# Keys of a gated recurrence transposed by VectorE blocks and a way through DRAM, not by TensorE

## The chip, the cores and the metric

The kernel runs on one core of one Trainium2 chip. Its metric is the device time of one execution in microseconds. The runs shown here and the profile are of that one core; the profile is of one execution, taken by the hardware profiler.

## The reference

One layer of a streaming encoder on a sequence of 2048 positions with 1024 channels, in float32:

```python
xn = rmsnorm(x, norm1_g)
u_pool, zq, zf, zi, zo, zg = split(xn @ w_in)          # 512 columns each, zg 2048
gates = sigmoid(zg + b_gate)
ya = pool_mixer(u_pool, pool_w, pool_scale) @ w_pa      # causal means over 2, 4, 8, 16 positions
yb = hgrn2_mixer(zq, zf, zi, zo, lower_bounds, g) @ w_pb
x = x + (gates[0] * ya + gates[1] * yb) @ w_o
x = x + conv_glu_ffn(rmsnorm(x, norm2_g), w_up, conv_w, conv_b, w_down)
return rmsnorm(x, final_g)
```

The change is in `hgrn2_mixer`, a linear recurrence with four heads of 128 channels and a forget gate f per position and channel:

```python
q = silu(zq); f = lb + (1 - lb) * sigmoid(zf); k = 1 - f; v = zi
S_t = diag(f_t) S_(t-1) + k_t^T v_t                     # S is 128 x 128
o_t = S_t^T q_t
```

It is computed in chunks of positions: inside a chunk by products of decayed q and k, from chunk to chunk through S. For the state, a chunk of 128 positions adds the matrix product of its decayed keys and its values, summed over the positions. Then o is normalised per head and multiplied with silu(zo).

## The kernel before, in words

**Projections.** Nearly all of TensorE's time is in large products (line 149), which are done in parts by a fast matrix scheme: a unit of four output tiles has the banks `X`, `Z` and `V` of PSUM, into which products of sums and differences of blocks go. Each product is done three times, with the high and low parts of both operands (`x_f6h`, `x_f6l`), and a matmul has 512 columns. ACT and DVE make the two parts of each weight tile (`ops`, lines 245 and 246); DVE takes the sums out of the banks (`gr_u` from `gr_Z`, line 1234, and so on), after which a bank is written again.

**Stages.** The sequence is worked in two halves (b = 0 and 2), each with two blocks of 512 positions. For each half come the input projection, the two branch projections, the output projection, and after both the feed-forward layer. The recurrence runs beside the input projection's units: `hgrn_task` is a Python generator, called for 4 blocks and 4 heads (16 times). Three runners work through the queue of such tasks. After every six projection matmuls the program takes a tick, in which each waiting generator counts down; `yield 4` means four ticks. So the recurrence's small products lie between projection matmuls in the program's order. A scheduler then fixes each engine's order once, when the kernel is built, by its own estimate of times; on the chip each engine goes strictly through its list and waits where an operand isn't there.

**A head.** A tile is 128 partitions by 512 elements, four chunks (`NT = 4`) of 128 positions. In `ks` the 128 channels lie on the partitions and the positions along the row. Levels of doubling (lines 1051 to 1127) multiply q, k and f and fill the matrix `att` inside the chunk. Then the keys are needed with positions on the partitions, since the state's product sums over them: TensorE transposes each chunk of `ks` into the bank `pk` (line 1131) by a product with the identity, and ACT copies the bank to `kt` (1133). The state products `pv` (line 1140) have a chunk of `kt` as the stationary operand, loaded into the array, and the chunk of `vt` as the moving one. An FP32 product takes two passes. DVE makes the states `ss` one after the other (line 1148), the last of a block into `st`. The outputs `po` sum the product inside the chunk (`v`, `att`, line 1156) and that of the state (`st` or `ss`, `q`, line 1158). Lines 1163 to 1178 normalise, transpose back (`pt`) and store (`od`).

**Queues.** SP issues all loads of weights (`raw`, line 198), the stores of combined weights (`wb<-cw`, line 983, rows of 512 bytes, two of 128 KB each; `kw..<-raw`), and the loads of heads (`v`, `z`, line 999). `spill` stores from ACT's queue, and `fetch` (lines 990 to 993) loads by default from SP's. At the end of a half the pooled channels come back as `mx` (line 992), and DVE makes the parts of `mf..` from them (lines 681 and 1503).

Of the kernel before, what the change touches and what calls it, by code (L numbers as in the profile page):

```python
# [11 lines left out]
F32 = mybir.dt.float32  # L12
# [6 lines left out]
P = 128  # L19
# [10 lines left out]
TB = 512  # L30
NT = TB // P
# [51 lines left out]
def tile_trunk(  # L83
# [16 lines left out]
    pe, act, dve, pool, sp = nc.tensor, nc.scalar, nc.vector, nc.gpsimd, nc.sync  # L100
# [6 lines left out]
    dram = ctx.enter_context(tc.tile_pool(name="dram", bufs=1, space=bass.MemoryType.DRAM))  # L107
    banks = ctx.enter_context(tc.tile_pool(name="banks", bufs=8, space=bass.MemoryType.PSUM))

    def slot(name, cols=TB, dt=F32):  # L110
        return slots.tile([P, cols], dt, tag="s", name=name, padded_shape=[P, 528])

    def bank(name, cols=512):
        return banks.tile([P, cols], F32, tag="b", name=name, padded_shape=[P, 512])
# [470 lines left out]
    ident = const.tile([P, P], F32, tag="ident", name="ident")  # L585
# [404 lines left out]
    def fetch(d, name, eng=sp):  # L990
        t = slot(name)
        eng.dma_start(t, d)  # L992
        return t


    def hgrn_task(b, h, d, q, vd, zd, od):
        def head_of(src, key):
            t = slot(f"{key}{b}_{h}")
            sp.dma_start(t.rearrange("p (c v) -> p c v", c=NT), src[:, :, h * P : (h + 1) * P])
            return t  # L1000

        vt = head_of(vd, "v")
        ks = slot(f"k{b}_{h}")
# [78 lines left out]
        for lv in (0, 1, 2, 4, 6):  # L1082
# [42 lines left out]
            dve.tensor_tensor(k3[:, :, 0, :], k3[:, :, 0, :],  # L1125
                              d3[:, :, 1, 0:1].to_broadcast(full), ALU.mult)
            dve.tensor_tensor(d3[:, :, 0, 0:1], d3[:, :, 0, 0:1], d3[:, :, 1, 0:1], ALU.mult)
        yield 4
        pk = bank(f"pk{b}_{h}")
        for c in range(NT):  # L1130
            pe.transpose(pk[:, c * P : (c + 1) * P], ks[:, c * P : (c + 1) * P], ident)
        kt = slot(f"kt{b}_{h}")
        act.copy(kt, pk)
        yield 4
        while (b, h) not in state_at:
            yield 1
        zt = head_of(zd, "z")
        pv = bank(f"pv{b}_{h}")
        for c in range(NT):
            pe.matmul(pv[:, c * P : (c + 1) * P], kt[:, c * P : (c + 1) * P],  # L1140
                      vt[:, c * P : (c + 1) * P], start=True, stop=True)
        ss = slot(f"ss{b}_{h}")
        par = b % 2
# [32 lines left out]
        t = slot(f"oh{b}_{h}")  # L1176
# [224 lines left out]
    def mixer(b0, forms, late):  # L1401
# [16 lines left out]
        def runner():  # L1418
            while taken[0] < 2 * HEADS:
                if queue:  # L1420
                    taken[0] += 1
                    yield from hgrn_task(*queue.pop(0))
                else:
                    yield 1
# [575 lines left out]
```

## Time and profile before

| What | Value |
|---|---|
| Time, median of 3 runs | 2505.35 us (2504.9 to 2505.46) |
| Span of the profiled execution, first to last instruction | 2503.3 us |
| Mean granted TensorE clock | 0.999 |
| TensorE busy | 2490.4 us (99%), 11428 matmul instructions |
| VectorE busy | 1977.8 us (79%) |
| ScalarE busy | 1201.1 us (48%) |
| GpSimd busy | 805.1 us (32%) |
| Transposes of the keys, line 1131 | 64, from 170.2 to 1661.6 us |
| State products, line 1140 | 128 passes, from 176.7 to 1676.3 us |

The profile's page gives the busy time of each engine, the chain that ended last, groups of instructions by line, and the DMAs with their time from issue to landing. TensorE's matmuls are pipelined: what one costs is the distance from its start to the next start, which the timelines show, and not its duration. In a name such as `pv<-v,kt` the tile ahead of the arrow is written, those behind are read. A row of waits says which engine stood idle at which line for whom: microseconds in all, times, the longest.

### The profile page before, as it was taken

How to read it: one execution, taken by the hardware profiler on the slowest of the kernel's cores; microseconds unless marked ns; L12 is line 12 of the kernel's file. 1: busy time of each engine (PE TensorE's matmuls, PEld its weight loads, DVE VectorE, ACT ScalarE, POOL GpSimd, SP SyncE). 2: the span in 40 equal slices, each digit the busy share in tenths (PEclk: the TensorE clock that was granted, in tenths of full speed). 3: DMA queues.
4: the chain of work that ended last, by engine and by line, in shares of the span. 5: the costliest groups of instructions: out<-in, count | busy, mean ns of one | idle time of the engine just before them, and what ended most of it. 6: DMA issues, size and time to landing. Idle time of an engine off the chain costs nothing.

```text
span 2503.3 us, 35640 instructions
## 1 busy us (share of the span) xinstructions
PE 2490.4 (99%) x11428; PEld 2039.1 (81%) x11428; DVE 1977.8 (79%) x3510; ACT 1201.1 (48%) x2264; POOL 805.1 (32%) x1139
## 2 busy tenths in 40 slices
PE   9999999999999999999999999999999999999998
PEld 7888888888888888888888888887888888888887
DVE  7778768997998778885596777679979887778755
ACT  6534443435555545553554344443365555445534
POOL 4343353403354333451320202223033433325410
PEclk9999999999999999999999999999999999999999
DMA  8888788688888789897344343447443454447852
GB/s 276 271 206 247 227 229 242 210 243 251 202 255 238 226 228 243 263 366 244 122 152 152 118 127 110 143 141 259 135 148 122 153 150 138 149 137 247 319 165 100
DMA packets 257691, 497.68 MB, mean 199 GB/s; under 512 B 26912, under 2 KB 47520, under 8 KB 257184
## 3 DMA queue, kind: packets, MB, share of 16 engines
q1 hardware_dynamic: 189872, 317.53, 40.0%
q0 software_dynamic: 42656, 112.74, 17.7%
q10 hardware_dynamic: 24976, 65.13, 7.5%
q8 instruction: 90, 1.47, 0.2%
q14 instruction: 97, 0.79, 0.1%
HBM read 383.63 MB, written 189.27 MB: 229 GB/s over the span
## 4 chain that ended last, share of the span: by engine, by line
PE 97%; DVE 1%; ACT 0%; DMA 0%; issue 0%; POOL 0%; SPq 0%; ACTq 0%; DVEq 0%
PE dn_P L149 17%; PE up_Z L149 15%; PE up_X L149 10%; PE up_V L149 10%; PE wo_P L149 6%; PE gr_Z L149 5%; PE gr_X L149 4%; PE gr_V L149 4%; PE pb L149 4%; PE io_Z L149 3%; PE fr_Z L149 3%; PE fr_X L149 2%; PE fr_V L149 2%; PE io_V L149 2%; PE pl L1057 2%; PE ur_Z L149 1%
## 5 line engine op out<-in xcount | busy, mean ns | idle before, releaser
L245 ACT CAST ops<-raw 128x512 fp32r<-128x512 f32 x792 | 489.3, 621 | 826.4 <-PE dn_P L149 176.6
L246 DVE TENSOR_TENSOR ops<-raw,ops 128x512 fp32r<-128x512 f32 x792 | 590.4, 749 | 202.8 <-ACT ops L245 198.4
L1734 DVE SCALAR_TENSOR_TENSOR e<-h,cols,e 128x512 f32<-128x512 f32 x176 | 143.4, 819 | 30.9 <-ACT e L1732 23.7
L1732 ACT ACTIVATE e<-h,cols 128x512 f32<-128x512 f32 x176 | 142.2, 814 | 25.1 <-DVE h L1190 18.2
L1737 DVE SCALAR_TENSOR_TENSOR e<-h,cols,e 128x512 f32<-128x512 f32 x176 | 134.0, 771 | 2.5
L992 POOL DMA_DIRECT2D g_P<-dg_P x154 | 83.8, 545 | 160.7 <-PE dn_P L149 112.1
L1303 POOL TENSOR_TENSOR gf_P<-e,e 128x512 f32<-128x512 f32 x44 | 61.1, 1391 | 149.4 <-DVE e L1743 95.9
L467 POOL TENSOR_TENSOR raw<-raw,raw 128x512 f32<-128x512 f32 x36 | 49.1, 1363 | 157.6 <-DVE ops L246 124.5
L1303 POOL TENSOR_TENSOR gf_P<-gf_P,e 128x512 f32<-128x512 f32 x44 | 59.2, 1345 | 71.8 <-DVE e L1743 71.4
L1727 POOL COPY h<-h 128x2 f32<-128x2 f32 x88 | 40.5, 472 | 117.3 <-DVE h L1189 110.4
L1443 POOL TENSOR_TENSOR q<-q,qs 128x512 f32<-128x512 f32 x16 | 22.1, 1380 | 166.3 <-ACT qs L1442 163.9
L1741 ACT ACTIVATE e<-e 128x512 f32<-128x512 f32 x88 | 55.6, 632 | 39.6 <-DVE e L1737 39.3
L1729 POOL COPY hist<-h 128x2 f32<-128x2 f32 x88 | 35.3, 402 | 118.9 <-DVE h L1190 117.1
L1190 DVE TENSOR_TENSOR h<-up_u,up_V 128x512 f32<-128x512 f32 x88 | 60.1, 683 | 10.2 <-PE up_V L149 9.7
L1278 DVE TENSOR_TENSOR x<-x,wo_P 128x512 f32<-128x512 f32 x88 | 56.0, 684 | 6.7 <-PE wo_P L149 6.3
L1476 ACT ACTIVATE gt<-gt,cols 128x512 f32<-128x512 f32 x48 | 34.9, 726 | 53.1 <-DVE gt L1190 39.5
L1278 DVE TENSOR_TENSOR ac<-ac,dn_P 128x512 f32<-128x512 f32 x72 | 47.1, 683 | 16.7 <-PE dn_P L149 16.3
L1042 POOL COPY qm<-q 128x64 f32<-128x64 f32 x64 | 27.1, 446 | 98.4 <-DVE q L1048 19.9
L1228 ACT COPY up_e<-up_X 128x512 f32<-128x512 f32 x44 | 25.8, 587 | 59.5 <-PE up_X L149 52.3
L1727 POOL COPY h<-hist 128x2 f32<-128x2 f32 x88 | 45.1, 519 | 28.5 <-DVE m_T42l L681 28.5
L1757 POOL DMA_DIRECT2D dg_P<-gf_P x88 | 50.7, 576 | 8.1 <-POOL gf_P L1303 7.4
L1057 PE MATMUL pl<-qm,k 128*128 128x192 f32 x256 | 50.0, 325 | 0.0
(1335 smaller groups left out, 8061.8 us busy)
## 6 DMA issues: line engine op xcount, KB each, us to landing
g_P<-dg_P POOLq DMA_DIRECT2D x154, 256.0 KB, 6.2
raw<-in_w_up_t SPq DMA_DIRECT2D x132, 256.0 KB, 3.3
raw<-in_w_in_t SPq DMA_DIRECT2D x98, 256.0 KB, 3.6
dg_P<-gf_P POOLq DMA_DIRECT2D x88, 256.0 KB, 4.0
dg_P<-e SPq DMA_DIRECT2D x66, 256.0 KB, 3.5
raw<-in_w_dn SPq DMA_DIRECT2D x66, 256.0 KB, 3.8
x<-in_x SPq DMA_DIRECT2D x64, 256.0 KB, 5.2
gd<-gt ACTq DMA_DIRECT2D x64, 256.0 KB, 2.7
```

The source lines that it names most:

```text
L149: count[1] = pe.matmul(*args, **kw)
L245: self.mark = act.copy(hi, v)
L246: low = self.low = dve.tensor_tensor(lo, v, f32(hi), ALU.subtract)
L992: eng.dma_start(t, d)
L1057: ins = pe.matmul(pa_[:, c * 192 : c * 192 + 192], ks[:, (i + c) * P : (i + c + 1) * P], mv[:, c].rearrange("p s x -> p (s x)"), start=Tru ...
L1190: return dve.tensor_tensor(dst, t, ps, ALU.add if how == "add" else ALU.subtract)
L1278: dve.tensor_tensor(t, t, ps[j], ALU.add if sg > 0 else ALU.subtract)
L1303: pin(eng.tensor_tensor(t, x0, x1, op))
L1727: pool.tensor_copy(h[:, 0:2], hist[:, mt] if hf == 0 else hs[s, 0][:, TB : TB + 2])
L1732: in_turn(act.activation(t, h[:, 2:], AF.Identity, bias=col(o_cb + mt), scale=col(o_cw + 4 * MF + mt)))
L1734: in_turn(second(dve.scalar_tensor_tensor(t, h[:, 1 : 1 + TB], col(o_cw + 2 * MF + mt), t, ALU.mult, ALU.add)))
L1737: dve.scalar_tensor_tensor(t, h[:, 0:TB], col(o_cw + mt), t, ALU.mult, ALU.add)
```

## The change

`pk` and the copy to `kt` go. In their place:

1. `blocks_turned`: one DVE instruction transposes the tile in blocks of 32x32, 64 blocks in a tile. It reads runs of 32 and writes with a stride of four elements (16 bytes), so that one chunk's blocks lie in every fourth element.
2. `blocks_moved`: four DMAs on SP's queue store the tile to a new DRAM tile `kd`, 64 KB each, a group of 32 partitions at a time, in runs of 512 bytes. The rows are put so that the DRAM tile holds the full transpose.
3. `fetch`: one DMA on SP's queue loads `kd` as `kt`, 256 KB in rows of 2 KB. The view `"p (m c) -> p c m"` takes chunk c as every fourth element.
4. The state product's stationary operand is `kt[:, c]`: 128 elements, 16 bytes from one to the next. The moving operand is the same as before.

The ticks around it are 2, 2, 2 and 3 in place of 4 and 4. In all 16 heads: 64 transposes of TensorE and 16 copies of ScalarE out, 16 transposes of VectorE and 80 DMAs on SP's queue (64 stores, 16 loads) in.

```diff
--- before.py
+++ after.py
@@ -993,6 +993,19 @@
         return t
 
 
+    def blocks_turned(t, name):
+
+        z = slot(name)
+        dve.transpose(z.rearrange("p (b j c) -> p b c j", b=4, c=NT),
+                      t.rearrange("p (c b i) -> p b c i", c=NT, b=4))
+        return z
+
+    def blocks_moved(dst, z, eng=sp):
+
+        d = dst.rearrange("(b i) (a m) -> a i b m", b=4, a=4)
+        for a in range(4):
+            eng.dma_start(d[a], z[32 * a : 32 * a + 32].rearrange("i (b m) -> i b m", b=4))
+
     def hgrn_task(b, h, d, q, vd, zd, od):
         def head_of(src, key):
             t = slot(f"{key}{b}_{h}")
@@ -1125,19 +1138,20 @@
             dve.tensor_tensor(k3[:, :, 0, :], k3[:, :, 0, :],
                               d3[:, :, 1, 0:1].to_broadcast(full), ALU.mult)
             dve.tensor_tensor(d3[:, :, 0, 0:1], d3[:, :, 0, 0:1], d3[:, :, 1, 0:1], ALU.mult)
-        yield 4
-        pk = bank(f"pk{b}_{h}")
-        for c in range(NT):
-            pe.transpose(pk[:, c * P : (c + 1) * P], ks[:, c * P : (c + 1) * P], ident)
-        kt = slot(f"kt{b}_{h}")
-        act.copy(kt, pk)
-        yield 4
+        yield 2
+        kz = blocks_turned(ks, f"kz{b}_{h}")
+        yield 2
+        kd = dram.tile([P, TB], F32, tag=f"kd{b}_{h}", name=f"kd{b}_{h}")
+        blocks_moved(kd, kz)
+        yield 2
+        kt = fetch(kd, f"kt{b}_{h}").rearrange("p (m c) -> p c m", c=NT)
+        yield 3
         while (b, h) not in state_at:
             yield 1
         zt = head_of(zd, "z")
         pv = bank(f"pv{b}_{h}")
         for c in range(NT):
-            pe.matmul(pv[:, c * P : (c + 1) * P], kt[:, c * P : (c + 1) * P],
+            pe.matmul(pv[:, c * P : (c + 1) * P], kt[:, c],
                       vt[:, c * P : (c + 1) * P], start=True, stop=True)
         ss = slot(f"ss{b}_{h}")
         par = b % 2
```

The orders of the engines move with it. The names: a number behind `pv`, `kt`, `ss`, `po` is the block and the head (`pv1_3` is block 1, head 3); `gr0_7_Z` is a bank of the last unit of the input projection, `mf0..` and `mx..` the pooled channels. Lines behind 1008 are 13 or 14 higher in the changed kernel (1140 is 1154, 1148 is 1162, 1156 and 1158 are 1170 and 1172, 1234 is 1248, 1503 is 1517).

First TensorE at the end of the first half's input projection, before, from the last head's state product on. Behind the last of these rows follow 21 more of line 149, then the remaining `po` products, the first of which reads `ss`:

```order
L1140 MATMUL pv0_3_4656<-v0_3_4057,kt0_3_4582 128x128 x4
L149 MATMUL gr0_7_V_4631<-x1_T13l_774,ops130_4511 128x512
L149 MATMUL gr0_7_V_4631<-x1_T13h_773,ops130_4511 128x512
L1156 MATMUL po0_3_4727<-v0_3_4057,at0_3_4062 128x128
L1158 MATMUL po0_3_4727<-st3_0_128,q0_3_4018 128x128
L1156 MATMUL po0_3_4727<-v0_3_4057,at0_3_4062 128x128
L1140 MATMUL pv1_3_4747<-v1_3_4071,kt1_3_4589 128x128 x2
L149 MATMUL gr0_7_Z_4595<-x1_T30h_819,ops131_4541 128x512
```

The same place of TensorE after:

```order
L149 MATMUL gr0_7_X_4579<-x0_f7h_419,ops132_4584 128x512
L1154 MATMUL pv0_3_4685<-v0_3_4069,kt0_3_4639 128x128 x4
L1170 MATMUL po0_3_4756<-v0_3_4069,at0_3_4074 128x128
L1172 MATMUL po0_3_4756<-st3_0_128,q0_3_4030 128x128
L1170 MATMUL po0_3_4756<-v0_3_4069,at0_3_4074 128x128
L1154 MATMUL pv1_3_4776<-v1_3_4083,kt1_3_4641 128x128 x4
L1172 MATMUL po0_3_4756<-ss0_3_4690,q0_3_4030 128x128
L1170 MATMUL po0_3_4756<-v0_3_4069,at0_3_4074 128x128
L1172 MATMUL po0_3_4756<-ss0_3_4690,q0_3_4030 128x128
L1170 MATMUL po0_3_4756<-v0_3_4069,at0_3_4074 128x128
L1172 MATMUL po0_3_4756<-ss0_3_4690,q0_3_4030 128x128
L149 MATMUL gr0_7_Z_4607<-x1_T40h_902,ops133_4612 128x512
```

Both heads' state products stand behind the last matmul of `gr0_7_X`, and no projection matmul is left between them, the `po` products that read `ss`, and the next write of `gr0_7_Z`. The second half's end has the same rows.

VectorE there, before, from the pooled parts to the read of `gr0_7_Z` by `u3`:

```order
L681 TENSOR_TENSOR mf0B110l_4645<-mx0_0_4605,mf0B110h_4644 128x512
L1148 SCALAR_TENSOR_TENSOR ss0_3_4661<-st3_0_128,f0_3_3995,pv0_3_4656 128x128
L1148 SCALAR_TENSOR_TENSOR ss0_3_4661<-ss0_3_4661,f0_3_3995,pv0_3_4656 128x128
L681 TENSOR_TENSOR mf0B111l_4667<-mx0_1_4607,mf0B111h_4666 128x512
L1503 TENSOR_TENSOR mf0_t10_4679<-mx1_0_4609,mx0_0_4605 128x512
L1148 SCALAR_TENSOR_TENSOR ss0_3_4661<-ss0_3_4661,f0_3_3995,pv0_3_4656 128x128
L1503 TENSOR_TENSOR mf0_t20_4681<-mx1_2_4611,mf0_t10_4679 128x512
L1148 SCALAR_TENSOR_TENSOR st3_1_129<-ss0_3_4661,f0_3_3995,pv0_3_4656 128x128
L681 TENSOR_TENSOR mf0T20l_4684<-mf0_t20_4681,mf0T20h_4683 128x512
L1234 TENSOR_TENSOR gr0_7_u3_4695<-gr0_7_Z_4595,gr0_7_e1_4593 128x512
```

And after:

```order
L681 TENSOR_TENSOR mf0B110l_4661<-mx0_0_4617,mf0B110h_4660 128x512
L681 TENSOR_TENSOR mf0B111l_4671<-mx0_1_4619,mf0B111h_4670 128x512
L1162 SCALAR_TENSOR_TENSOR ss0_3_4690<-st3_0_128,f0_3_4007,pv0_3_4685 128x128
L1517 TENSOR_TENSOR mf0_t10_4695<-mx1_0_4621,mx0_0_4617 128x512
L1162 SCALAR_TENSOR_TENSOR ss0_3_4690<-ss0_3_4690,f0_3_4007,pv0_3_4685 128x128
L1517 TENSOR_TENSOR mf0_t20_4697<-mx1_2_4623,mf0_t10_4695 128x512
L1162 SCALAR_TENSOR_TENSOR ss0_3_4690<-ss0_3_4690,f0_3_4007,pv0_3_4685 128x128
L1162 SCALAR_TENSOR_TENSOR st3_1_129<-ss0_3_4690,f0_3_4007,pv0_3_4685 128x128
L681 TENSOR_TENSOR mf0T20l_4700<-mf0_t20_4697,mf0T20h_4699 128x512
L1248 TENSOR_TENSOR gr0_7_u3_4711<-gr0_7_Z_4607,gr0_7_e1_4605 128x512
```

The same instructions stand between the first `ss` and the read of `gr0_7_Z`, in nearly the same order; the two `mf0_t` sums now lie between the first and the third `ss`, one place earlier than before.

SP's queue at the same place, after; the rows of `kd` are four DMAs each:

```order
L1007 DMA kd0_3_4593<-kz0_3_4568 32x4x128 x4
L1007 DMA kd1_3_4598<-kz1_3_4570 32x4x128 x4
L198 DMA raw107_4615<-wb13_3316 128x512
L992 DMA mx0_0_4617<-md0_0_2011 128x512
L992 DMA mx0_1_4619<-md0_1_2151 128x512
L992 DMA mx1_0_4621<-md1_0_2067 128x512
L992 DMA mx1_2_4623<-md1_2_3936 128x512
L992 DMA mx1_1_4625<-md1_1_2177 128x512
L992 DMA mx1_3_4627<-md1_3_4020 128x512
L992 DMA mx0_2_4629<-md0_2_3864 128x512
L992 DMA mx0_3_4631<-md0_3_3997 128x512
L992 DMA kt0_3_4639<-kd0_3_4593 128x512
```

The load of the last heads' keys stands behind the eight loads of `mx`, which were there before too.

## The prediction, made before the changed kernel ran

> **What bounds the kernel now.** I read the page's head and chain first, then the waits of TensorE (PE), then the table of stages.
>
> ```profile
> span 2503.3 us, 35640 instructions
> PE 2490.4 (99%) x11428; PEld 2039.1 (81%) x11428; DVE 1977.8 (79%) x3510; ACT 1201.1 (48%) x2264; POOL 805.1 (32%) x1139
> ...
> PE x_t L744 <- DVE x_xs L738: 2.9, 4, 1.1
> PE warm L706 <- POOL ident L587: 1.4, 1, 1.4
> PE pa_Z L149 <- DVE pa_u L1230: 0.9, 2, 0.5
> PE io_Z L149 <- ACT ops L245: 0.6, 1, 0.6
> ...
> 125.00:500.00 375.00, 374.57 (x1873) 310.75 (x1872) 301.14 (x698) 158.31 (x351) 165.14 (x168) 1.00 0.78 227
> 1375.00:1750.00 375.00, 374.55 (x1885) 312.99 (x1884) 291.28 (x699) 155.39 (x343) 85.05 (x102) 1.00 0.47 149
> ```
>
> PE is busy 99% of the span and waits 5.8 us in all (2.9 + 1.4 + 0.9 + 0.6). The last two rows (PE, PEld, DVE, ACT, POOL busy, clock, DMA share, GB/s) are the two stages in which the recurrence runs: PE has no gap there, and VectorE (DVE) is second at 301 and 291 of 375 us. So every PE pass removed is won whole, every PE pass that gets longer is lost whole, and whatever another engine gives to PE later than before is a new gap. The span is 2503.3 us and the median of the runs 2505.35, so 2.05 us are added to a span.
>
> **Removed: 64 transposes.**
>
> ```profile
> 170.01 0.40 PE L149 MATMUL fr_X<-x_f3l,ops 128*128 128x512 f32 x1
> 170.24 1.04 PE L1131 MATMUL pk<-ident,k 128*128 128x128 f32 x8
> 171.04 0.48 PE L149 MATMUL fr_X<-x_f3h,ops 128*128 128x512 f32 x1
> 171.35 0.40 PE L149 MATMUL fr_Z<-x_T20h,ops 128*128 128x512 f32 x1
> ...
> L1131 PE MATMUL pk<-ident,k x64: 270/272/273, 170.2 to 1661.6; 128*128 128x128 f32 x64
> L1133 ACT COPY kt<-pk x16: 585/587/594, 170.9 to 1662.0; 128x512 f32<-128x512 f32 x16
> ```
>
> The first four rows are PE's timeline (start, us), the last two the groups of the tile pk (fastest, median, slowest ns). Matmuls are pipelined, so their price is the distance of starts, not the 272 ns of one. A projection matmul steps by 0.23 us (170.01 to 170.24). From 170.24 to 171.35 lie eight transposes and one such matmul: 1.11 − 0.23 = 0.88 us, 0.11 us for one transpose. 64 × 0.11 = **7.0 us** off PE. The 16 copies of ScalarE (16 × 0.587 = 9.4 us) end nothing on PE's path, since that engine is busy 158 of 375 us.
>
> **Changed: 128 passes with a strided stationary tile.** The state products are the same in number, but their stationary operand `kt[:, c]` is now 128 elements with 16 bytes from one to the next. No stationary operand of the kernel before has a stride, so there is no row of it. The nearest rows are VectorE's, where the products of f by f (L1127) run with strides: first its groups by line and shape from 1375 to 1750 us (busy us, mean ns of one), then PE's timeline at a pv.
>
> ```profile
> L1048 DVE TENSOR_TENSOR q<-qm,f 128x128 f32<-128x128 f32 x32 | 8.6, 285 | 0.4 <-ACT qm L1041 0.4
> ...
> L1127 DVE TENSOR_TENSOR f<-f 128x256 f32<-128x256 f32 x6 | 2.5, 422 | 0.1
> L1016 DVE TENSOR_TENSOR q<-q,f 128x256 f32<-128x256 f32 x6 | 2.5, 420 | 0.4 <-ACT f L1004 0.4
> ...
> L1127 DVE TENSOR_TENSOR f<-f 128x128 f32<-128x128 f32 x6 | 2.4, 394 | 0.1
> ...
> 176.67 1.05 PE L1140 MATMUL pv<-v,kt 128*128 128x128 f32 x8
> 177.48 0.48 PE L149 MATMUL fr_V<-x_T13h,ops 128*128 128x512 f32 x1
> 177.80 0.38 PE L1156 MATMUL po<-v,at 128*128 128x128 f32 x2
> ```
>
> 128 columns in runs of four or more take 285 ns (L1048). From 128 to 256 columns at a stride of 8 bytes it is 422 − 285 = 137 ns more, 1.07 ns an element, as for plain data. But 128 columns at 16 bytes (L1127, `"p (b t h)"` with t = h = 2) take 394: 109 ns more for the same number, almost a second time for each element. So VectorE pays nothing at 8 bytes and nearly double at 16, the stride of the new weight load. The eight pv passes cost 177.80 − 176.67 − 0.23 = 0.90 us, 0.11 each, in which PE streams 128 columns and loads 128 others beside it. With 0.109 more for the load, a pass is paced by it at about 0.22. The first load of a group of eight lies beside a 0.23 us projection matmul and is hidden, so seven of eight count: 112 × 0.109 = **+12.2 us**. The ends are 0 (PE's load reads in its own way, and a slower array load is no certainty) and 128 × 0.11 = +14.1 (each load doubled). I take the L1127 row: it is the one row with this stride.
>
> [...]
>
> **Added: the way of the keys.** 16 VectorE transposes, 64 stores of 64 KB and 16 loads of 256 KB on SP's queue. The nearest VectorE price is 0.69 us for 128x512 (next fence), and 0.69 + 512 × 109/128 ns = 1.12 if its writes at 16 bytes cost what L1127 says.
>
> ```profile
> 167.05 0.69 DVE L1190 TENSOR_TENSOR u<-ur_u,ur_V 128x512 f32<-128x512 f32 x1 [0.76 <-PE ur_V L149]
> 182.87 0.39 PE L149 MATMUL fr_X<-x_f6h,ops 128*128 128x512 f32 x1
> ...
> 168.52 1.24 SPq L983 DMA_DIRECT2D wb<-cw  x2
> 422.49 4.89 SPq L992 DMA_DIRECT2D mx<-md  x8
> ...
> v<-vd SPq DMA_DIRECT2D x16, 256.0 KB, 4.3
> ...
> raw<-wb SPq DMA_DIRECT2D x16, 256.0 KB, 3.3
> ...
> wb<-cw SPq DMA_DIRECT2D x16, 128.0 KB, 5.0
> ```
>
> Timelines of DVE, PE and SP, then the page's list of DMAs (KB each, us from issue to landing). The first pair of heads, where the way is tightest: in the new order its two turns stand before the u of 167.05, so they end by about 168.5. The 512-byte rows of wb are the like of the stores: 0.62 us of issue each (1.24/2) and 5.0 to land. Four stores, two wb and four stores issue in 6.2 us: the first head's last store issues at 171.0 and lands at 176.0, its fetch (4.3, as v<-vd) at 180.3; the second's store at 174.7, landed 179.7, its fetch 184.0. The new pv stands behind fr_X's f6, 182.87 before, less the eight transposes and the eight pv passes that stood ahead of it (1.8): 181.1. The second pv stands behind the first, three projection matmuls and three po products: 0.9 to 1.7, and 1.4 us later, 183.4 to 184.2. Both just hold. With 3.3 for the fetch (raw<-wb) a whole microsecond is to spare; half a microsecond each more and every pair of heads waits about one. At the end of the pass the fetch stands behind eight mx loads that were issued by 427.4, so it lands near 432.5, and pv, now behind gr_X's f7, comes after that. I take **+1 us**, from 0 to 8 (1 us for each of eight pairs).
>
> VectorE gains 16 × 0.69 to 1.12 = 11 to 18 us in 750 where it has 158 idle. That fits, but some evictions that PE awaits come one turn later. At pa_Z PE already waits for VectorE twice, so there a turn goes through: 2 × 1 = **+2 us** (0 to 4).
>
> **Moved: the end of each pass.** The order shows pv of the last head behind the matmuls that covered its chain; PE's and DVE's timelines of before at that place:
>
> ```profile
> 430.57 0.38 PE L1156 MATMUL po<-v,at 128*128 128x128 f32 x2
> 430.79 0.39 PE L1158 MATMUL po<-st,q 128*128 128x128 f32 x2
> ...
> 430.69 0.35 DVE L1148 SCALAR_TENSOR_TENSOR ss<-ss,f,pv 128x128 f32<-128x128 f32 x1
> ...
> 431.98 1.78 DVE L1503 TENSOR_TENSOR mf_t<-mx,mx 128x512 f32<-128x512 f32 x1
> ...
> 433.94 1.53 DVE L1503 TENSOR_TENSOR mf_t<-mx,mf_t 128x512 f32<-128x512 f32 x1
> 435.40 0.33 DVE L1148 SCALAR_TENSOR_TENSOR st<-ss,f,pv 128x128 f32<-128x128 f32 x1
> 436.17 1.03 DVE L681 TENSOR_TENSOR mf0T20l<-mf_t,mf0T20h 128x512 fp32r<-128x512 f32 x1 [0.43 <-ACT mf0T20h L680]
> 437.12 0.68 DVE L1234 TENSOR_TENSOR gr_u<-gr_Z,gr_e 128x512 f32<-128x512 f32 x1
> 438.44 0.68 DVE L1503 TENSOR_TENSOR mf_t<-mx,mx 128x512 f32<-128x512 f32 x1
> ```
>
> Before, 22 projection matmuls (22 × 0.23 = 5.1 us) lay between pv and the po that needs ss, so this VectorE chain cost nothing. After, PE has from pv's end to the next projection only eight po products (0.22 each, 430.57 to 430.79: 1.76 us) and the second pv (0.9, or 1.7 with slow loads), 2.7 to 3.4 us. That projection writes the bank gr_Z, which must wait until gr_u (L1234) has read it. The chain to there: three ss and st at 0.35 (1.4), two mf_t (1.78 + 1.53, or 0.68 each as at 438.44), the wait of 0.43, L681 1.03, gr_u 0.68: 6.9 us as timed before, 4.5 with the short forms and no wait. PE stands still for 1.1 us (4.5 − 3.4) to 4.2 (6.9 − 2.7). With slow loads and the mean of both chains it is 5.7 − 3.4 = 2.3. The second pass has the same rows: **+4.6 us**, 2 to 8.
>
> **Sum.** −7.0 + 12.2 + 1 + 2 + 4.6 = +12.8: span 2516.1, and with 2.05 a time of **2518 us**. With slow loads, the ends of the other three terms give −7.0 + 12.2 + 0 + 0 + 2 = +7.2 and −7.0 + 14.1 + 8 + 4 + 8 = +27; since they don't all come together, its own range is 2512 to 2524.
>
> **Rivals.** (a) The stride costs PE nothing. Then −7.0 + 1 + 2 + 2 × (5.7 − 2.7) = +2.0: 2507, from 2501 to 2511. [...] Against it: L1127.
> (b) The gain arrives: no stride price, and VectorE's short forms leave the pass ends short. −7.0 + 0 + 2 × 1 = −5: 2500, or 2498 with none. This needs two favours at once, against the 1.78 and 1.53 us rows.
> (c) The keys come late everywhere: the fetches on SP's queue, with 80 more DMAs on it, land 3 us later than the rows say, which is from the point of half a microsecond on a wait of each pair: 8 × 2.5 = 20 in place of the 1, 2537; with 1.5 us, 2525. For it: a DMA share of 0.78 in the first pass. Against it: 0.47 in the second, and 256 KB loads of the same queue that land in 3.3 to 4.3 us.
> (d) What the change says doesn't happen: the order removes L1131 and L1133 on PE and ACT, so this one is out.
>
> **Chances.** The sum 0.53; (a) 0.27; (b) 0.11; (c) 0.09. A difference below 0.2% (5 us: 2500.3 to 2510.4) can't be told from none. Faster is (b): 0.11. The same is (a) but for its upper edge, and the lowest edge of the sum: 0.27. Slower: 0.62. The range leaves out the half of (b) and (c): 2500 to 2524; the likeliest case's own is 2512 to 2524.
>
> **What would show it.** Right: starts of pv passes 0.2 us or more apart, where before eight of them and a projection take 1.13 us; new rows of PE waiting for ss and gr_u at about 437 and 1680, 2 us each; no row of pv waiting for a DMA. Wrong: pv passes still at 0.11 (then (a) or (b), told apart by the waits at the pass ends), or pv waiting for kt (then (c)), or waits for VectorE elsewhere that together pass 4 us.

## The result, and the profile after

| | before | after |
|---|---|---|
| Time, median (range) | 2505.3 us (2504.9 to 2505.46) | 2528.59 us (2524.6 to 2530.66) |
| Ratio, 95% interval | 1 | 1.0091 (1.0079 to 1.0103) |
| Span of the profiled execution | 2503.3 us | 2526.4 us |

The change costs 23.3 us. The forecast was 2518 us, from 2500 to 2524: slower was right, the size was not. The measured time lies above the range. The changed kernel's times also spread over 6 us, ten times as far as the first four of the kernel before.

TensorE's waits in the changed kernel (microseconds in all, times, the longest), with the head of its page:

```profile
span 2526.4 us, 35647 instructions
...
PE 2502.0 (99%) x11364; PEld 2049.2 (81%) x11364; DVE 1987.5 (79%) x3526; ACT 1195.1 (47%) x2248; POOL 799.7 (32%) x1139
...
PE pa_Z L149 <- DVE pa_u L1244: 4.6, 3, 2.2
PE pv L1154 <- issue: 3.5, 1, 3.5
PE x_t L744 <- DVE x_xs L738: 3.3, 4, 1.4
PE warm L706 <- POOL ident L587: 1.4, 1, 1.4
PE fr_Z L149 <- DVE fr_u L1244: 0.9, 1, 0.9
PE pl L1110 <- ACT q L1027: 0.9, 1, 0.9
PE wo_P L149 <- DVE x L1292: 0.6, 1, 0.6
PE pv L1154 <- DMA kt<-kd: 0.6, 1, 0.6
PE io_Z L149 <- ACT ops L245: 0.6, 1, 0.6
PE gr_Z L149 <- DVE gr_u L1248: 0.5, 2, 0.2
PE pv L1154 <- DMA kwg3ins<-raw: 0.3, 1, 0.3
```

PE waits 17.2 us where it waited 5.8: 11.4 more. That it is 99% busy and its busy time even grew by 11.6 us shows the rest: its instructions got longer. The groups of the tile kt in the changed kernel (fastest, median, slowest ns):

```profile
L1154 PEld LDWEIGHTS pv<-v,kt x128: 307/329/332, 185.7 to 1695.6; 128*128 128x128 f32 x128
...
DMA to landing us min/median/max: 2.5/4.1/8.8
```

The weight load of a state product takes 329 ns (192 before). And the first pair of heads, in PE's timeline:

```profile
181.85 0.40 PE L149 MATMUL fr_X<-x_f6h,ops 128*128 128x512 f32 x1
185.75 2.21 PE L1154 MATMUL pv<-v,kt 128*128 128x128 f32 x8 [3.51 <-issue]
187.61 0.77 PE L149 MATMUL fr_X<-x_f7h,ops 128*128 128x512 f32 x1
188.19 0.63 PE L149 MATMUL fr_X<-x_f7l,ops 128*128 128x512 f32 x1
188.61 0.63 PE L149 MATMUL fr_X<-x_f7h,ops 128*128 128x512 f32 x1
...
190.14 2.03 PE L1154 MATMUL pv<-v,kt 128*128 128x128 f32 x8
192.00 0.39 PE L1172 MATMUL po<-ss,q 128*128 128x128 f32 x2
```

Three things are in these lines. Eight pv passes take 1.86 us (190.14 to 192.00), 0.23 each, where they took 0.11. The first pv waits 3.5 us for its keys: its row names no releaser, but the one fetch that SP issues from 176.8 to 177.2 us lands 8.8 us later, at 185.7 (KB, us from issue to landing):

```profile
kt<-kd SPq DMA_DIRECT2D x1, 256.0 KB, 8.8
```

And after the wait a projection matmul steps by 0.42 us (188.19 to 188.61) in place of 0.23: the clock is at half. The stretches around it (PE, PEld, DVE, ACT, POOL busy, granted clock, DMA share, GB/s), and those around the wait at pa_Z in the first half:

```profile
183.11:186.52 3.41, 0.77 (x3) 0.80 (x4) 0.00 (x0) 0.00 (x0) 0.00 (x0) 1.00 0.77 247
186.52:189.93 3.41, 3.41 (x14) 3.12 (x14) 1.93 (x5) 0.00 (x0) 0.00 (x0) 0.50 0.42 134
189.93:193.35 3.42, 3.42 (x21) 3.35 (x21) 1.59 (x4) 1.69 (x3) 0.50 (x1) 1.00 0.87 299
...
466.42:469.83 3.41, 1.27 (x7) 0.73 (x5) 3.33 (x5) 1.21 (x2) 2.49 (x2) 1.00 1.05 346
469.83:473.24 3.41, 3.41 (x8) 2.73 (x9) 2.72 (x7) 1.26 (x3) 0.38 (x1) 0.50 1.00 362
```

Twice the clock is at 0.50 for 3.41 us, each time behind a stretch in which PE was mostly idle (busy 0.77 and 1.27 of 3.41 us). Beside these it is low only at the end of the program (0.50 from 2521.24 us on), as before (0.50 from 2498.63). A stretch at half clock loses at most half its length, 1.7 us; the first loses less, since the eight strided pv passes that run into it took 1.86 us there too (185.75 to 187.61). So the account is: strided loads, taken alone in the first run below, +15.0; transposes −7.0; waits +11.4; clock at most 2 × 1.7 = +3.4. That is at most 22.8 of the 23.1 us between the two spans.

### The profile page after: what moved, and what is told of

It is laid out like the page before. It is cut to its first block, busy times and chain, and to the rows that moved or that the text cites. A ratio compares the mean times of both kernels' runs of the same rounds, so it can differ in the third digit from the quotient of the medians.

```text
span 2526.4 us, 35647 instructions
## 1 busy us (share of the span) xinstructions
PE 2502.0 (99%) x11364; PEld 2049.2 (81%) x11364; DVE 1987.5 (79%) x3526; ACT 1195.1 (47%) x2248; POOL 799.7 (32%) x1139
## 4 chain that ended last, share of the span: by engine, by line
PE 94%; DVE 3%; DMA 2%; issue 1%; ACT 1%; SPq 0%; POOL 0%; ACTq 0%; DVEq 0%
PE dn_P L149 17%; PE up_Z L149 15%; PE up_X L149 10%; PE up_V L149 10%; PE wo_P L149 5%; PE gr_Z L149 5%; PE pb L149 4%; PE gr_X L149 3%; PE gr_V L149 3%; PE io_Z L149 3%; PE fr_Z L149 2%; PE io_V L149 2%; PE pl L1070 2%; PE fr_X L149 2%; PE fr_V L149 2%; PE ur_Z L149 1%
```

## The experiments

Times are medians, each beside the kernel before on the same chip.

| Run | Time, us | Before beside it | Ratio (95%) |
|---|---|---|---|
| e1_stride16 | 2519.94 | 2504.97 | 1.0060 (1.0045 to 1.0075) |
| e1b_stride8 | 2506.20 | 2504.97 | 1.0005 (0.9996 to 1.0015) |
| e2_actcopy | 2523.94 | 2504.97 | 1.0077 (1.0062 to 1.0092) |
| e3_later | 2525.01 | 2504.97 | 1.0083 (1.0066 to 1.0100) |
| e4_way8 | 2518.55 | 2505.71 | 1.0049 (1.0034 to 1.0064) |
| e5_way8_early | 2521.07 | 2505.71 | 1.0061 (1.0044 to 1.0077) |
| e6_both | 2528.82 | 2505.71 | 1.0090 (1.0075 to 1.0105) |
| e7_private | 2519.87 | 2504.91 | 1.0063 (1.0046 to 1.0079) |
| e7_private_later | 2518.77 | 2504.91 | 1.0052 (1.0037 to 1.0067) |
| e7_control | 2511.18 | 2504.91 | 1.0025 (1.0014 to 1.0036) |
| e8_half1 | 2518.46 | 2504.94 | 1.0049 (1.0034 to 1.0064) |
| e8_half2 | 2507.99 | 2504.94 | 1.0011 (1.0002 to 1.0020) |
| e8_half2_h012 | 2503.34 | 2504.94 | 0.9992 (0.9984 to 1.0001) |
| e9_quiet | 2503.36 | 2505.25 | 0.9994 (0.9985 to 1.0003) |
| e9_quiet_more | 2502.00 | 2505.25 | 0.9989 (0.9980 to 0.9998) |

### The stride alone

The kernel before, with only the layout of `kt` changed:

```diff
-        act.copy(kt, pk)
+        kt = kt.rearrange("p (m c) -> p c m", c=NT)
+        act.copy(kt, pk.rearrange("p (c m) -> p c m", c=NT))
...
-            pe.matmul(pv[...], kt[:, c * P : (c + 1) * P],
+            pe.matmul(pv[...], kt[:, c],
```

> The kernel before with its TensorE transposes and ScalarE copies, but the copy writes kt so that a chunk takes every fourth element, and the state products load it with 16 bytes from one element to the next. No VectorE transpose and no way through DRAM. Theory S (the strided load doubles a pass): the steps inside a group of eight pv passes go from 0.11 to about 0.21 us, 128 x 0.107 = 13.7 us less a hidden first load in some groups, so 2517 to 2520. Rival R (the long steps of the changed kernel come from late keys or the clock, not from the stride): steps stay 0.11 and the time is 2505 to 2507.

And with two chunks interleaved, so that the stride is 8 bytes:

```diff
-        act.copy(kt, pk)
+        kt = kt.rearrange("p (x m c) -> p x c m", x=2, c=2)
+        act.copy(kt, pk.rearrange("p (x c m) -> p x c m", x=2, c=2))
```

> As the run before, but a chunk takes every second element: 8 bytes from one to the next, two elements in each 16 bytes. [...] Rival (any stride costs the load): steps of 0.15 to 0.21, 2511 to 2520.

The loads of the first with PE's timeline at its first pv, and then the loads of the second:

```profile
L1141 PEld LDWEIGHTS pv<-v,kt x128: 307/329/332, 176.0 to 1690.0; 128*128 128x128 f32 x128
...
176.22 1.90 PE L1141 MATMUL pv<-v,kt 128*128 128x128 f32 x8
177.88 0.48 PE L149 MATMUL fr_V<-x_T13h,ops 128*128 128x512 f32 x1
```

```profile
L1141 PEld LDWEIGHTS pv<-v,kt x128: 193/196/199, 176.3 to 1677.7; 128*128 128x128 f32 x128
```

At 16 bytes a load takes 329 ns and the kernel 15.0 us more; at 8 bytes 196 ns (192 without a stride) and 1.2 us, which the interval doesn't tell from nothing. Theory S holds at 16 bytes and both rivals fall, the second by 2506.2 against its 2511 to 2520: with one element in 16 bytes the stride costs, with two it doesn't; no other stride was tried. No wait is new in the first run (its 0.9 at pa_Z is that of before), so its 15.0 us are the price of 128 loads, 0.117 each in the mean. A group of eight that stands behind a projection matmul goes from 0.81 us (176.67 to 177.48 before) to 1.66 (176.22 to 177.88), seven times 0.12; four of its groups stand behind a po product and take 1.78, eight times 0.12 more. ScalarE's copy, which writes kt, pays in the same way: 1.09 us at 16 bytes and 0.62 at 8, against 0.59 without a stride.

### The stride undone in the changed kernel

```diff
-        kt = fetch(kd, f"kt{b}_{h}").rearrange("p (m c) -> p c m", c=NT)
-        yield 3
+        kf = fetch(kd, f"kf{b}_{h}").rearrange("p (m c) -> p c m", c=NT)
+        yield 2
+        kt = slot(f"kt{b}_{h}").rearrange("p (c m) -> p c m", c=NT)
+        act.copy(kt, kf)
+        yield 1
```

> The changed kernel with one part undone: the tile that comes back from DRAM is copied by ScalarE into a second tile whose chunks are contiguous, and the state products load that. Theory S: the changed kernel less about 14 us, so 2512 to 2518, with pv steps of 0.11 and the waits for late keys and at pa still there. Rival R (the stride isn't to blame): 2525 to 2531 as the changed kernel.

The loads are back at 192 ns, but only 4.7 of the 14 us came back, and the time lies between the two ranges that were written. TensorE now waits for the copy, and for VectorE behind it:

```profile
PE pv L1157 <- ACT kt L1150: 6.5, 3, 3.3
PE pa_Z L149 <- DVE pa_u L1247: 3.7, 3, 2.2
...
PE gr_Z L149 <- DVE gr_u L1251: 3.0, 4, 1.2
```

Its granted clock was 0.996 in the profiled run and 0.998 in that of the change; 0.002 of its span of 2522.2 us, some 5 us, is an estimate of what that costs more. The copy, which reads at 16 bytes, takes 1.11 us each (0.59 the copy out of the bank in the kernel before) and stands in the path of the keys, so this run mixes two things. The next takes the 8-byte layout along the whole way instead, with nothing added to the path:

```diff
+        for x in range(2):
+            half = slice(256 * x, 256 * x + 256)
+            dve.transpose(z[:, half].rearrange("p (b j c) -> p b c j", b=4, c=2),
+                          t[:, half].rearrange("p (c b i) -> p b c i", c=2, b=4))
...
+        d = dst.rearrange("(b i) (x a m) -> a i x b m", b=4, x=2, a=4)
...
+        kt = fetch(kd, f"kt{b}_{h}").rearrange("p (x m c) -> p x c m", x=2, c=2)
```

> The changed kernel with pairs of chunks interleaved in place of all four: the turned tile, the DRAM tile and kt hold a chunk in every second element, so that writes and weight loads run at 8 bytes; the stores have runs of 256 bytes in place of 512, the turn is two instructions of 256 columns. Theory S: pv steps of 0.11 us, so 14 us less than the changed kernel, 2511 to 2517, as nothing is added to the path of the keys. Rival M (PE only comes sooner to the same waits, and the faster passes turn into waiting, as the run with the ScalarE copy lost 10 of its 14 us): 2520 to 2526.

2518.6: 10 us less than the change, not 14, between the theory's range and the rival's. PE's waits grew from 17.2 to 19.6 us and the granted clock of the profiled run fell from 0.998 to 0.997, so part of the gain turned into waiting; that PE now comes sooner to the same late keys is the likely reason, not a shown one. Against the kernel before it still loses 12.8 us, though 64 transposes are gone: the way itself costs some 20.

### More time for the keys

```diff
         kt = fetch(kd, f"kt{b}_{h}").rearrange("p (m c) -> p c m", c=NT)
-        yield 3
+        yield 8
```

> The changed kernel with eight ticks in place of three between the load of the keys and the state products; the strided load stays. Theory W (the rest of the loss, some 9 us, is waiting for late keys at the first heads, what VectorE does late behind it, and the halved clock after the wait): pv's wait of 3.5 us and the 1.7 us of halved clock after it go, 2518 to 2524. Rival (the waits only move, to the end of the pass and to pa): 2526 to 2532.

3.6 us less, just outside both ranges that were written (2518 to 2524 and 2526 to 2532) and within the spread of the runs of the change. The first pv still waits 2.5 us, and new waits stand at gr_Z (2.6 and 2.1): the waits mostly moved.

```diff
-        yield 2
         kz = blocks_turned(ks, f"kz{b}_{h}")
-        yield 2
+        yield 1
...
         blocks_moved(kd, kz)
-        yield 2
+        yield 1
         kt = fetch(...)          # 8-byte layout
-        yield 3
+        yield 10
```

> The run before with the turn at once (no ticks ahead), one tick to the stores, one to the load, and ten from there to the state products in place of three. Theory W (what is left is late keys, the halved clock behind them, and VectorE's lateness behind those): PE's waits for kt go and it comes near the kernel before or below, 2499 to 2508. Rival P (the tiles that the way holds and VectorE's extra work set the waits wherever the state products stand): over 2512.

2521.1, no better than e4_way8 and far from the 2499 to 2508 of theory W, that the loss is a matter of giving the keys time. The run is no clean case of it, since the keys still come late once: with ten ticks PE waits for ACT's weights (3.2 us), for keys (3.0), and for `ss` (2.5). The next run settles it.

### The way without anyone who waits for it

The kernel before with its own transposes, and the whole way beside it into a tile that nothing reads:

```diff
         act.copy(kt, pk)
-        yield 4
+        kz = blocks_turned(ks, f"kz{b}_{h}")
+        yield 2
+        kd = dram.tile([P, TB], F32, tag=f"kd{b}_{h}", name=f"kd{b}_{h}")
+        blocks_moved(kd, kz)
+        yield 2
+        kf = fetch(kd, f"kf{b}_{h}")
```

> The kernel before with TensorE's transposes and its own kt, and beside them the whole way (16 turns, 64 stores, 16 loads) into a tile that no one reads. Theory W (the loss beside the stride is that the state products wait for the way): nobody waits, 2505 to 2508. Rival P (VectorE's 17 us more, tiles held until the stores land, and the transfers themselves cost as much): 2511 to 2518.

It loses 23.1 us, more than either side had written, with contiguous weight loads and no wait for keys: theory W falls. Its waits of PE, then of VectorE, and VectorE's timeline at the first pair:

```profile
PE pa_Z L149 <- DVE pa_u L1248: 8.0, 2, 4.4
PE fr_Z L149 <- DVE fr_u L1248: 7.7, 2, 5.8
...
DVE p L961 <- DMA kd<-kz: 8.7, 2, 5.8
DVE ss L1166 <- DMA kd<-kz: 3.9, 2, 3.0
...
182.95 0.69 DVE L961 SCALAR_TENSOR_TENSOR p<-s,u 128x512 f32<-128x512 f32 x1 [5.78 <-DMA kd<-kz]
...
184.46 0.68 DVE L1248 TENSOR_TENSOR fr_u<-fr_e,fr_Z 128x512 f32<-128x512 f32 x1
```

Here is a wait that the prediction didn't have. In this kernel, as in the changed one, the next tile in the place of the first `kz` is `p`, an output of the pooling branch that has nothing to do with the keys. So `p` can't be written until the four stores of `kz` have landed; VectorE took the two in the order of its list, and behind `p` (182.95 us) stands `fr_u` (184.46), for which PE waits. PE's wait for that `fr_u` is the 5.8 us of the second row. In the changed kernel the same row of VectorE reads 4.6 us, and PE's wait behind it 0.9 (fr_Z, at 177.15 us). This run holds more tiles than the changed kernel, as `kt` of its own is there beside `kz` and `kf`, so it may overstate the cost. TensorE's granted clock was 0.995 in the profiled run, the lowest of the profiled runs here.

### Tiles of their own

The 8-byte layout with two tiles for `kz` that nothing else uses. To make room there are 76 common tiles in place of 77, and 7 raw weight tiles in place of 8:

```diff
-N_SLOTS = 77
+N_SLOTS = 76
-N_RAW = 8
+N_RAW = 7
+    turned = ctx.enter_context(tc.tile_pool(name="turned", bufs=2))
...
-        z = slot(name)
+        z = turned.tile([P, TB], F32, tag="kz", name=name)
```

> The version with 8-byte strides, with two tiles of their own for the turned keys, so that no other tile takes the place of one whose stores haven't landed. Room for them: 76 common tiles in place of 77 and 7 in place of 8 for raw weights. Theory H (VectorE's queue stands behind a tile that a store still holds, as its rows of p and ss waiting for kd<-kz show, and that is the main loss beside the stride): those rows go, and the time falls from 2518.6 to 2509 to 2514. Rival K (late keys at the state products and the halved clock behind them are the main loss): 2516 to 2520, with no rows of VectorE waiting for kd<-kz all the same.

> The run before with six ticks in place of three between the load of the keys and the state products. Theory H with the waits for keys covered too: 2499 to 2508, the 7 us of the transposes nearly won. Rival (the state products come late for what follows them, as in the run with eight ticks and shared tiles, which won 3 us): 2510 to 2518.

The kernel before with only the two pool sizes changed:

> The kernel before with 76 common tiles and 7 for raw weights, nothing else. If the smaller pools cost nothing, 2504 to 2507, and the two runs beside it can be read against the kernel before. If they cost, by that much the two must be read lower.

No row of VectorE waiting for kd<-kz is left in e7_private (in e4_way8 there were 2.3 us of them; with six ticks one of 2.8 stands at `fr_u`), and the time is that of e4_way8, within rival K's range. But the control alone loses 6.3 us, and read lower by that much, as was written beforehand, e7_private is at 2513.6, within theory H's range. Nor is that reading safe: the control's longest new wait (3.7 us for weights at io_V) is 0.5 in e7_private, so its loss isn't simply contained there. So theory H stays open by these runs. The one with six ticks lies just above both its ranges, or lowered alike, at 2512.5, in its rival's, and it spread over 8.6 us. What replaced the waits is plain: PE waits 10.4 us for kt (5.9 the longest), and with six ticks 5.5 us. The control does show that one common and one raw tile fewer cost 6.3 us in this kernel.

### By half and by head

If not the tiles and not the ticks, then the place. The transfers of the changed kernel, first from 160 to 450 us, then from 1375 to 1700 (KB each, median us from issue to landing):

```profile
kd<-kz SPq DMA_DIRECT2D x32, 64.0 KB, 4.1
kt<-kd SPq DMA_DIRECT2D x8, 256.0 KB, 4.5
```

```profile
kd<-kz SPq DMA_DIRECT2D x32, 64.0 KB, 2.1
kt<-kd SPq DMA_DIRECT2D x8, 256.0 KB, 4.1
```

The stores take twice as long in the first half, the fetches hardly longer. At the very first pair they took 6.3 and 7.9 us and the fetch 8.8 (from 165 to 185 us the DMA engines' share is 1.05, with a 1024 KB load from GpSimd's queue among them); at 1420 to 1436 us the share is 0.45. The kernel before had 0.91 from 165 to 190 us too, so the way met full engines there and didn't fill them. So the 8-byte way was run in a part of the heads only, the others with TensorE (in these three runs also with 8-byte strides):

```diff
+        if b < 2:                 # e8_half1; b >= 2: e8_half2; b >= 2 and h < 3: e8_half2_h012
             yield 2
             kz = blocks_turned(ks, f"kz{b}_{h}")
...
+        else:
+            yield 4
+            pk = bank(f"pk{b}_{h}")
...
```

> The way of the keys with 8-byte strides for the first half of the sequence alone (8 heads); the second half's keys by TensorE and ScalarE as before, also with 8-byte strides. Theory C (the loss beside the stride comes where the way meets the full DMA engines of the first half, share 0.8 to 1, against 0.4 to 0.5 in the second): nearly all of the 13 us that the way with 8-byte strides lost over the kernel before is here, 2513 to 2520, with waits for keys or kd at about 185 us. Rival D (each half loses alike, at its end): 2510 to 2513.

> The way with 8-byte strides for the second half of the sequence alone, the first half by TensorE. Theory C: 32 transposes less are 3.5 us, against some 2 us of waiting at the end of the half; 2502 to 2507. Rival D: 2509 to 2513.

> The way with 8-byte strides for heads 0 to 2 of the second half alone; the last head, whose products stand at the half's end, by TensorE as all of the first half. Theory C and the wait at pa as a matter of the last head: no new wait is left, 24 x 0.11 = 2.6 us off, 2502 to 2504. Rival (the way disturbs VectorE wherever it runs): 2505 to 2510.

First half alone: +13.5 us. Second alone: +3.1. Second without its last head: −1.6, not clear of nothing. New waits of PE in e8_half1, then in e8_half2:

```profile
PE pv L1166 <- issue: 7.7, 3, 3.1
...
PE pa_Z L149 <- DVE pa_u L1256: 2.8, 3, 2.2
PE pl L1112 <- ACT q L1029: 1.5, 2, 1.1
```

```profile
PE pa_Z L149 <- DVE pa_u L1256: 2.6, 2, 2.2
PE pv L1166 <- DMA kt<-kd: 1.5, 1, 1.5
...
PE gr_Z L149 <- DVE gr_u L1260: 1.1, 1, 1.1
```

The equal halves of rival D fall, theory C holds for where the loss is: 13.5 against 3.1, though 2508.0 lies 1 us above its range, and the two losses together are more than the 12.8 of e4_way8. Rival D was right in part. In e8_half2 PE's waits in the second half all lie at its end (1669 to 1695 us, 4.8 us); in e8_half1 6.7 us lie at the end of the first half (420 to 520 us), 5.3 at the first pair, and 1.9 between; the granted clock of its profiled run was 0.998, that of e8_half2's 0.999. Without the last head of the second half none is left there: pa_Z is at 0.9 again. So the stalls at that end belong to the last head, which this run shows; its late place in TensorE's order is the likely reason. In e8_half1 VectorE has no wait for kd<-kz at all, so its 13.5 us don't come from VectorE standing at a held tile (ScalarE stood 3.4 us for one there, GpSimd 2.7); PE's longest waits are at pv. That the first half loses by the full DMA engines is shown only so far: the runs locate it, the landing times fit, but no run emptied the engines there.

### The way in a part of the heads alone

Heads 0 to 2 of the second half by the 8-byte way, all others exactly as in the kernel before; then head 1 of the first half as well:

```diff
+        if b >= 2 and h < 3:                       # e9_quiet
+        if b >= 2 and h < 3 or b < 2 and h == 1:   # e9_quiet_more
```

> The way with 8-byte strides for heads 0 to 2 of the second half; all other heads exactly as in the kernel before, with kt contiguous. Theory C: 24 transposes less are 2.6 us and no wait comes, so 2502 to 2503 against the kernel before beside it at 2505; that is at the edge of what can be told apart. Rival (the way costs VectorE and the queues something everywhere): 2504 to 2507.

> The same, and head 1 of the first half by the way too, where the half-one run showed no wait from 230 to 330 us: 32 transposes less, 3.5 us, 2501 to 2502. Rival: a new wait of 1 to 4 us in the first half, 2503 to 2506.

The second is 3.25 us faster than the kernel before, close to the 3.5 of 32 transposes less, with an interval just clear of 1; the first, 1.9 us faster, has one that isn't. The second's waits of PE:

```profile
PE x_t L744 <- DVE x_xs L738: 3.1, 2, 2.2
PE warm L706 <- POOL ident L587: 1.4, 1, 1.4
PE pa_Z L149 <- DVE pa_u L1257: 0.8, 2, 0.4
PE io_Z L149 <- ACT ops L245: 0.6, 1, 0.6
PE io_V L149 <- ACT ops L245: 0.2, 1, 0.2
```

They are those of the kernel before: 6.1 us in all. So the way adds no wait where it is covered, and the time agrees with 0.11 us for a transpose as the timeline said; the interval (0.5 to 5 us) can't fix that price.

## Why the prediction was right or wrong

Slower was right, and the largest term had the right mechanism. The step that failed most is what PE waits, 7.6 us in three terms, and how they are made up. The trace shows 11.4 us of new waits: 4.4 at pv (+1 was taken), 5.5 at pa_Z, fr_Z and pl (+2), 0.5 at gr_Z (+4.6) and 1.0 elsewhere. By luck the 4.1 us too many at gr_Z hid over half of what the other two lacked. Behind the waits came up to 3.4 us of half clock, for which the sum had nothing, and the stride's term was 2.8 us too small. Together that is at most 10.0 of the 10.6 us between 2518 and 2528.6.

- **64 × 0.11 = 7.0 us off PE**: the runs agree. Where no new wait came with it, 32 transposes gave 3.25 us.
- **The strided load, +12.2, by VectorE's row at the same stride**: the mechanism was right and the term too small; it measured 15.0 alone. A load cost 0.12 us more and not VectorE's 0.109. That the first of a group is hidden held behind a projection matmul (0.85 us more for eight, seven times 0.12) and not behind a po product (0.97, eight times 0.12), nor for the groups of four (0.48 more). In e1_stride16 118 loads counted, not 112. The sum's upper end, each load doubled (14.1), was nearer.
- **VectorE's turn, 0.69 to 1.12 us**: 1.09 in the median, at the upper end, the one that counts its writes at 16 bytes by L1127.
- **Late keys, +1 us, "Both just hold"**: wrong. The first pv alone waited 3.5 us. The prices of landing, 5.0 and 4.3, were medians of the whole program, and were used for a stretch where the DMA engines' share is 1.05 (165 to 185 us); there stores took 6.3 and 7.9 and the fetch 8.8. The sum had that fetch from 176.0 to 180.3 us; it was issued at 176.9 and landed at 185.7, so its price is what failed, by 4.5 us. For the second pair the sum didn't hold by its own numbers unless the loads are slow: 184.0 against 183.4 to 184.2. That pair came without a wait.
- **VectorE's lateness, +2 us**: the place pa_Z was right, the mechanism was not. pa_Z went from 0.9 to 4.6, fr_Z and pl came new with 1.8. The 0.9 at fr_Z follows the 4.6 us that VectorE stood at a tile which a store still held. The stalls at pa_Z, 2.1 and 2.2, lie at the ends of the halves, over 35 us behind the last heads' turns, so they aren't a turn that goes through; the next point has what stands ahead of them. Of the prediction's own signs of being wrong, "waits for VectorE elsewhere that together pass 4 us" came.
- **The end of each pass, +4.6 us in two**: the rows of gr_Z waiting for gr_u came, at the place that was named, but with 0.5 us in all. VectorE's timeline of the changed kernel there:

```profile
447.42 0.35 DVE L1162 SCALAR_TENSOR_TENSOR ss<-st,f,pv 128x128 f32<-128x128 f32 x1 [5.61 <-PE pv L1154]
447.69 0.69 DVE L1517 TENSOR_TENSOR mf_t<-mx,mx 128x512 f32<-128x512 f32 x1
...
450.53 0.68 DVE L1248 TENSOR_TENSOR gr_u<-gr_Z,gr_e 128x512 f32<-128x512 f32 x1
```

  The chain ran in its short forms throughout, 3.8 us from 447.42 to the end of gr_u, where the sum took a mean with the long ones, 5.7. VectorE had idled 5.6 us before it, for the last head's pv, so nothing was in its way. That idle time is what the sum left out: VectorE stood at the `ss`, next in its order, and from 447.42 to the stall at pa_Z, whose `pa_u` it begins at 469.01, it was busy 20.5 of 21.6 us, with no time to catch up. At the other end it idled 4.7 us for pv, before 1693.59, and pa_Z stalled at 1715.98. In e8_half2_h012, where TensorE transposes the last head's keys, VectorE has no such wait from 1655 to 1700 us, and pa_Z no stall.
- **The clock**: no term for it, and no reason given for none. Two stretches at half clock cost up to 3.4 us; each wait had been priced at its own length.

Rival (c), the keys late, was given 0.09 and a condition at every pair; in the changed kernel it came true in earnest for the first pair alone (3.5 us; 0.6 and 0.3 elsewhere). (a) and (b) fell with the stride's price.

## What to carry to other kernels

A transpose off TensorE is worth only its steps, here 0.11 us by the timeline, so what replaces it must be covered on every queue that it touches: also by tiles, where a store that holds its source can make an unrelated writer wait (`p`, 4.6 us in the change and 5.8 in e6_both). Price a transfer from rows of the stretch it will run in, not from the program's median, and try such a way first in the parts of the program where the DMA engines are half idle: here the second half, with a share of 0.47 before, lost 3.1 us by the 8-byte way and the first, with 0.78, lost 13.5. A stationary fp32 operand with one element in 16 bytes cost 0.12 us a load here; pairs of chunks interleaved, two elements in 16 bytes, cost nothing that could be told from none.

## What the runs showed of the hardware

A wait of TensorE can cost more than its length. In the changed kernel the two stretches at half clock (0.50, 3.41 us each) begin at 186.52 and 469.83 us: 0.77 us behind the end of pv's wait of 3.51 us, and at the end of a wait of 2.14 us at pa_Z. But the wait of 2.15 us at pa_Z that ends at 1715.98 us has none behind it:

```profile
1715.98 0.47 PE L149 MATMUL pa_Z<-mf2T30h,ops 128*128 128x512 f32 x1 [2.15 <-DVE pa_u L1244]
```

That is a row of PE's timeline of the changed kernel. In the 3.41 us up to there PE was busy 1.26 us, against 1.27 up to 469.83, and the granted clock was 1.00 in the 3.41 us behind it, against 0.50. So two waits of one length differed by up to 1.7 us in price, the half of 3.41; what decides it is not shown. It may be part of why the kernels with such stalls spread over 2 to 9 us and the kernel before over 0.6 us in its first four runs and 2.4 in its widest series; that was not tried apart.
